# Ordering a whole diffusion step by the tile scheduler's other machine model

## The chip, the cores and the metric

The kernel runs on one NeuronCore of one Trainium2 chip. The metric is the device time of one execution in microseconds (us). Before the change the median of three runs is 1921.22 us (1920.97 to 1921.4). A difference under about 0.2% (3.8 us) counts as none.

## The reference, cut to what matters

One inference step of a two-layer backbone, for 128 context tokens and 512 latent tokens with the same weights, model width 1024. Layer 0 mixes tokens with a bidirectional state-space scan, layer 1 with differential attention; each is followed by a channel mixer of hidden width 2816.

```python
for i in range(DEPTH):                       # DEPTH = 2
    hp = modulate(xp, norm_mix_g[i], p_sh1, p_sc1)
    hs = modulate(xs, norm_mix_g[i], s_sh1, s_sc1)
    if i % N_MIXERS == 0:                    # scan in both directions, chunks of 128 tokens
        op, st = ssd_mixer(hp, h_zero, *ssd_p)
        os_, _ = ssd_mixer(hs, state_ssd[:, slot], *ssd_p)
    else:                                    # 8 heads, each with two softmax maps
        op = diff_out(diff_attend(qp, kp, vp, lam), att_subln_g[slot], att_out_w[slot], lam_init)
        os_ = diff_out(diff_attend(qs, k_all, v_all, lam), att_subln_g[slot], att_out_w[slot], lam_init)
    xp = xp + p_g1 * op
    xs = xs + s_g1 * os_
    xp = xp + p_g2 * conv_ffn(modulate(xp, norm_ffn_g[i], p_sh2, p_sc2), *ffn_p)
    xs = xs + s_g2 * conv_ffn(modulate(xs, norm_ffn_g[i], s_sh2, s_sc2), *ffn_p)
y = rmsnorm(xp, final_norm_g), rmsnorm(xs, final_norm_g)
```

## The kernel before, in words

**Layout.** Activations lie transposed in SBUF: 128 channels on the partitions, all 640 tokens (512 latent, 128 context) along the free axis, eight such tiles for the model width. A product with a weight matrix yields one output tile of 128 channels by 640 tokens at a time in PSUM, and each such tile has one "unit" of weights of at most 128 x 1024.

**Dense products.** A unit is loaded as float32 (`raw`, four buffers), then split in two float32r parts: ScalarE copies it to `whi` (L135), VectorE subtracts to get `wlo` (L136). Activations are split the same way. `dense_many` (L150 to L162) multiplies for every block of 128 input channels the three products hi x hi, hi x lo, lo x hi, each over two parts of the tokens, 256 columns ("A") and 384 columns ("B"), into the same PSUM tile. So a tile over eight blocks has 24 pairs of matmuls. `nextw` (L139) prefetches three units ahead and casts one unit ahead.

**Interleaving.** Everything that isn't a dense product is written as Python generators. `add` puts one in a list; `hook` (L75), called by `dense_many` after each block of input channels, moves those on that are due. What a generator yields is the number of hooks until it goes on. In this way the text of the program mixes the scan of a group, a head's attention, the norms and the modulation rows into the stream of dense products:

```python
for wt, x, s0, s1 in ((wh, h[k][0], st, False), (wh, h[k][1], False, False), (wl, h[k][0], False, sp)):
    for p in parts:
        c0, c1 = HALF[p]
        self.mm(ps[:m, COL0[p] + c0:COL0[p] + c1], wt, x[:, c0:c1], s0, s1)
self.hook()
```

**Stages, in the order of the text.**
- *Start* (`first_tiles`, L366): inputs, constants and the first modulation rows (`modp`, tiles `mp`, 32 transfers) are loaded on SP's queue; the first norm; the first three dense tiles.
- *Scan layer* (`ssd`, L836): for each of four groups six tiles x, B, C and four tiles z, with the scan of the group before (`ssd_group`, L669: transposes `xtp`, states `st`, decays `r`, outputs `yp`) mixed in; then the output projection `po`.
- *First channel mixer* (`ffn`, L521): 44 up tiles with a convolution over tokens on VectorE and ScalarE (`ca`, `cv`, `uraw`), then products `ml`, `mh`, and 24 down tiles `po` in three sub-blocks. `mod_rest` (L479) computes the modulation of layer 1 meanwhile, on VectorE: 48 tiles `mw` of weights are loaded and multiplied twice each (L501).
- *Attention* (`attention`, L1073): eight heads, each with dense tiles q, k, v; the scores `sl`, the softmax (`sm`, `e`) and the weighted sum (`wt`, `ov`) of one head are mixed into the dense tiles of the next. The output projection begins after six heads.
- *Second channel mixer*, as the first, without `mod_rest`; then the final norm and the stores (`final_task`, L1102).

**Who sets the order.** The text only gives a program order. When the context of L1273 closes, the tile scheduler makes of it one queue for each engine (PE, DVE, ACT, POOL and SP, which issues nearly all transfers). It plays the program on a machine model: whenever an engine of the model is free, it is given the earliest instruction in program order that the model says can run, which means that its data are there and a buffer for its result is free. The queues that come out are fixed, and semaphores are put where one engine must wait for another. On the chip each engine works its queue from the front. So an instruction that the model saw as ready sooner than the chip does holds up what stands behind it.

The lines that the prediction speaks of: L103 is every matmul but the transposes, L682 the transposes of the scan, L94 every ScalarE operation, L97 and L100 VectorE's, L123 the weight loads, L494 the loads `mw` and L501 the products made of them. Shapes tell them apart.

## Time and profile before

| | |
|---|---|
| median of three runs | 1921.22 us |
| the profiled execution's own time | 1921.78 us |
| its span, from the first to the last instruction | 1920.0 us |
| mean granted clock of TensorE | 0.993 |
| moved by DMA | 185.01 MB, mean 96 GB/s |
| DMA issues waiting longest on SP's queue | weight loads L123, 194 times, behind the cast that frees their buffer |

The profile's page gives for one execution the busy time of each engine, the chain of work that ended last, and the costliest groups of instructions. Besides it the trace answers questions by stage: how long each engine was busy between two moments, at which clock TensorE ran (1.00 is full), and on what an engine waited. A matmul's row names its output, then its moving and stationary operands by the program's names; a number with x is a count. "PEld" is TensorE's loading of stationary operands, which runs beside its matmuls. Matmuls overlap, so the mean duration of one is longer than the step from one to the next.

### The profile page before, as it was taken

The page shows a single profiled execution, that of the slowest core. Times are in us where ns is not written, and L with a number is a line of the kernel's source. Part 1 is how long each engine was busy: PE and PEld are TensorE (multiplying, and loading weights), DVE is VectorE, ACT ScalarE, POOL GpSimd, SP SyncE. Part 2 cuts the span into 40 slices and gives each one's busy share as a digit, 9 for nine tenths or more (in the row PEclk, how much of TensorE's full clock was granted, in tenths as well). Part 3 has the DMA queues.
Part 4 walks back from the last instruction along what each step waited for, and adds up shares of the span by engine and source line. Part 5 has one row for each costly group of instructions (what it writes and reads, how often), then busy time and mean ns, then how long its engine had stood idle before and what let it go on. Part 6 is the DMA issues. An engine that isn't in the chain of part 4 may idle for free.

```text
span 1920.0 us, 33586 instructions
## 1 busy us (share of the span) xinstructions
PE 1887.8 (98%) x13741; PEld 1781.4 (93%) x13741; DVE 1377.3 (72%) x2649; ACT 944.5 (49%) x1753; POOL 0.2 (0%) x4
## 2 busy tenths in 40 slices
PE   7999999999999999999999999999999999999997
PEld 4899898989989999999999989888899999999997
DVE  4779998989847999994455877788677553553554
ACT  3468585858525542343343566666446432441441
POOL 0000000000000000000000000000000000000000
PEclk9999999999999999999999999999999999999998
DMA  9612112123452556642222211111032222222211
GB/s 341 230 56 67 56 55 78 45 67 101 158 173 78 181 181 206 208 138 75 77 68 76 86 38 50 49 46 34 13 121 80 77 77 78 65 68 88 72 40 55
DMA packets 66730, 185.01 MB, mean 96 GB/s; under 512 B 8336, under 2 KB 14736, under 8 KB 66448
## 3 DMA queue, kind: packets, MB, share of 16 engines
q1 hardware_dynamic: 66000, 182.34, 29.3%
q8 instruction: 108, 1.77, 0.4%
q10 hardware_dynamic: 576, 0.52, 0.1%
q14 instruction: 46, 0.38, 0.1%
HBM read 177.06 MB, written 5.77 MB: 95 GB/s over the span
## 4 chain that ended last, share of the span: by engine, by line
PE 94%; DVE 2%; DMA 1%; ACT 1%; issue 0%; SPq 0%; DVEq 0%; ACTq 0%
PE up L103 30%; PE po L103 25%; PE z L103 6%; PE x L103 5%; PE st L103 5%; PE bc L103 3%; PE yp L103 3%; PE v L103 3%; PE q L103 2%; PE sl L103 2%; PE k L103 2%; PE ov L103 1%; PE modrow L103 1%; PE r L103 1%; PE wt L1052 1%; PE in L103 1%
## 5 line engine op out<-in xcount | busy, mean ns | idle before, releaser
L94 ACT ACTIVATE whi<-raw 128x1024 fp32r<-128x1024 f32 (+4 forms) x230 | 236.0, 1027 | 414.4 <-PE po L103 243.7
L100 DVE TENSOR_TENSOR wlo<-raw,whi 128x1024 fp32r<-128x1024 f32 (+4 forms) x230 | 270.3, 1177 | 183.8 <-ACT whi L94 178.1
L97 DVE SCALAR_TENSOR_TENSOR xr<-po,mod,xr 128x256 f32<-128x256 f32 (+2 forms) x231 | 89.0, 434 | 159.0 <-PE po L103 158.8
L103 PE MATMUL po<-mh,whi 128*128 128x256 f32 (+1 forms) x704 | 167.5, 310 | 0.0
L103 PE MATMUL po<-ml,whi 128*128 128x256 f32 (+1 forms) x704 | 167.2, 309 | 0.0
L103 PE MATMUL po<-mh,wlo 128*128 128x256 f32 (+1 forms) x704 | 167.0, 309 | 0.0
L103 PE MATMUL up<-h01h,wlo 128*128 128x256 f32 (+1 forms) x656 | 149.4, 308 | 0.0
L103 PE MATMUL up<-h11h,wlo 128*128 128x256 f32 (+1 forms) x656 | 149.4, 308 | 0.0
L103 PE MATMUL up<-h01h,whi 128*128 128x256 f32 (+1 forms) x656 | 149.3, 308 | 0.0
L103 PE MATMUL up<-h11h,whi 128*128 128x256 f32 (+1 forms) x656 | 149.3, 308 | 0.0
L103 PE MATMUL up<-h01l,whi 128*128 128x256 f32 (+1 forms) x656 | 149.3, 308 | 0.0
L103 PE MATMUL up<-h11l,whi 128*128 128x256 f32 (+1 forms) x656 | 149.3, 308 | 0.0
L103 PEld LDWEIGHTS po<-mh,whi 128*128 128x128 f32 x704 | 128.3, 188 | 0.6 <-ACT mh L94 0.4
L103 PEld LDWEIGHTS po<-mh,wlo 128*128 128x128 f32 x704 | 128.6, 188 | 0.0
L103 PEld LDWEIGHTS po<-ml,whi 128*128 128x128 f32 x704 | 128.4, 188 | 0.0
L103 PEld LDWEIGHTS up<-h01h,wlo 128*128 128x128 f32 x656 | 119.3, 188 | 0.0
L103 PEld LDWEIGHTS up<-h11h,wlo 128*128 128x128 f32 x656 | 119.3, 188 | 0.0
L103 PEld LDWEIGHTS up<-h11h,whi 128*128 128x128 f32 x656 | 119.3, 188 | 0.0
L103 PEld LDWEIGHTS up<-h01h,whi 128*128 128x128 f32 x656 | 119.3, 188 | 0.0
L103 PEld LDWEIGHTS up<-h01l,whi 128*128 128x128 f32 x656 | 119.3, 188 | 0.0
L103 PEld LDWEIGHTS up<-h11l,whi 128*128 128x128 f32 x656 | 119.2, 188 | 0.0
L97 DVE SCALAR_TENSOR_TENSOR ca<-uraw,fcw,ca 128x511 f32<-128x511 f32 (+1 forms) x176 | 85.2, 546 | 11.7 <-ACT ca L94 11.7
(505 smaller groups left out, 4469.2 us busy)
## 6 DMA issues: line engine op xcount, KB each, us to landing
raw<-in_w_up SPq DMA_DIRECT2D x88, 512.0 KB, 3.5
mw<-in_modT SPq DMA_DIRECT2D x48, 512.0 KB, 3.6
raw<-in_w_in SPq DMA_DIRECT2D x40, 512.0 KB, 3.5
raw<-in_w_dn SPq DMA_DIRECT2D x32, 448.0 KB, 3.3
raw<-in_w_qkv SPq DMA_DIRECT2D x24, 512.0 KB, 3.5
mr<-in_mod SPq DMA_DIRECT2D x44, 256.0 KB, 5.4
raw<-in_w_so SPq DMA_DIRECT2D x16, 512.0 KB, 4.1
raw<-in_w_dn SPq DMA_DIRECT2D x16, 512.0 KB, 3.7
```

Source lines behind the costliest of these rows:

```text
L94: return self.nc.scalar.activation(out, in_, func, **k)
L97: return self.nc.vector.scalar_tensor_tensor(out, in0, s, in1, op0, op1)
L100: return self.nc.vector.tensor_tensor(out, a, b, op)
L103: return self.nc.tensor.matmul(out, lhsT, rhs, start=start, stop=stop)
L1052: nc.tensor.transpose(pm[:, b * P:(b + 1) * P], ws[b][:, kc * P:(kc + 1) * P], self.ident)
```

## The change

The text of the kernel is the same. One argument of the context is set, which makes the scheduler play the program on its other machine model, a simulator of the time line of each engine and queue, in place of its default one. Both have durations and latencies of their own for each instruction and transfer; neither changes what is computed, the sizes of tiles or the number of buffers. Only the order in the five queues, which buffer of its set a tile gets, and the places of the semaphores can differ.

```diff
-    with tile.TileContext(nc) as tc:
+    with tile.TileContext(nc, schedule_with_timeline_sim=True) as tc:
         _emit(tc, **a)
```

## The prediction

> **What bounds the kernel now.** I read the page first (busy shares and the chain), then the busy time by stage, then what TensorE waited for, and last single places on the time line.
>
> ```profile
> span 1920.0 us, 33586 instructions
> PE 1887.8 (98%) x13741; PEld 1781.4 (93%) x13741; DVE 1377.3 (72%) x2649; ACT 944.5 (49%) x1753; POOL 0.2 (0%) x4
> PE 94%; DVE 2%; DMA 1%; ACT 1%; issue 0%; SPq 0%; DVEq 0%; ACTq 0%
> ```
>
> TensorE is busy in 1887.8 of 1920.0 us, and 94% of the chain that ended last is its own work. It is the bound, and 32.2 us is all that it stands idle. The profiled execution took 1921.8 us, 1.8 us more than its span; the median of the three timed runs is 1921.2 us, 0.6 us less than that, so a difference worked out in the trace is simply added to 1921.2.
>
> The next table has one row per stage (start, the scan layer, the first channel mixer, the hand-over to attention, attention with its projection, the second channel mixer, the end). Columns: length, busy time of TensorE, of its weight load, VectorE, ScalarE, GpSimd, then the granted clock, the DMA share and GB/s.
>
> ```profile
> 0.00:60.00 60.00, 48.05 (x501) 34.24 (x505) 31.77 (x67) 21.48 (x36) 0.20 (x4) 0.97 0.91 326
> 60.00:600.00 540.00, 538.43 (x4265) 485.76 (x4258) 451.88 (x905) 343.43 (x807) 0.00 (x0) 1.00 0.28 93
> 600.00:1054.00 454.00, 454.00 (x3129) 453.47 (x3127) 347.11 (x610) 179.21 (x229) 0.00 (x0) 1.00 0.42 134
> 1054.00:1080.00 26.00, 25.09 (x193) 23.82 (x194) 21.25 (x70) 12.50 (x27) 0.00 (x0) 1.00 0.23 66
> 1080.00:1440.00 360.00, 355.74 (x2443) 318.67 (x2442) 277.35 (x568) 208.93 (x427) 0.00 (x0) 0.99 0.17 54
> 1440.00:1900.00 460.00, 460.00 (x3152) 459.53 (x3150) 237.28 (x404) 178.13 (x226) 0.00 (x0) 1.00 0.21 67
> 1900.00:1920.00 20.00, 6.51 (x74) 5.90 (x72) 10.64 (x29) 0.83 (x2) 0.00 (x0) 0.70 0.38 132
> ```
>
> Of the 32.2 us idle, 11.95 lie in the first 60 us, where the DMA engines are 91% busy, and 13.49 in the last 20, where the final norm and the stores follow the last matmul. The two channel mixers, 914 us together, have no idle TensorE at all. What an order of instructions can own in the middle is 1.57 us in the scan layer, 0.91 at the hand-over and 4.26 in attention: 6.74 us.
>
> Short waits can cost more than they last. Same columns:
>
> ```profile
> 222.00:226.00 4.00, 3.21 (x21) 2.11 (x20) 3.98 (x7) 3.73 (x11) 0.00 (x0) 1.00 0.09 31
> 326.00:330.00 4.00, 3.21 (x21) 2.12 (x20) 4.00 (x6) 3.60 (x11) 0.00 (x0) 1.00 0.04 14
> 1362.00:1366.00 4.00, 2.20 (x13) 1.42 (x16) 2.88 (x7) 3.05 (x8) 0.00 (x0) 0.92 0.01 2
> 1366.00:1370.00 4.00, 4.00 (x25) 3.24 (x18) 3.33 (x10) 1.02 (x2) 0.00 (x0) 0.50 0.17 51
> 1370.00:1374.00 4.00, 4.00 (x22) 3.98 (x22) 1.95 (x7) 2.46 (x6) 0.00 (x0) 0.72 0.00 0
> 1110.00:1115.00 5.00, 4.34 (x20) 3.55 (x21) 4.60 (x10) 4.55 (x12) 0.00 (x0) 0.78 0.05 15
> 1115.00:1120.00 5.00, 5.00 (x33) 4.69 (x32) 4.18 (x8) 2.78 (x7) 0.00 (x0) 0.88 0.32 105
> ```
>
> Idle of 0.79 us near 224 and 328 left the granted clock at 1.00. Idle of 1.80 us near 1363 was followed by a clock of 0.50: 0.08 x 4 + 0.50 x 4 + 0.28 x 4 = 3.44 us of full clock lost, so that place cost 5.24 us. Near 1112, 0.66 us idle and 0.22 x 5 + 0.12 x 5 = 1.70 us of clock, 2.36 us. With 5.14 us of clock, the middle stages lose 6.74 + 5.14 = 11.9 us to places where TensorE stood waiting.
>
> **The change, part by part.** No instruction is added, dropped or resized: the same matmuls, casts and transfers come out in another order in the engines' queues, each still waiting for the same data and buffers. The scheduler gives each engine, whenever its model machine says the engine is free, the earliest instruction of the program text that the model says can run. Another model means other moments of "can run", so the order changes where engines compete, and where several jobs are open at once. That this is so already now shows inside one tile of the scan layer:
>
> ```profile
> 204.77 1.03 PE L682 MATMUL xtp<-cst,xf 128*128 128x128 f32 x8
> 205.56 0.54 PE L103 MATMUL x<-h00h,whi 128*128 128x256 f32 x2
> 208.99 0.28 PE L103 MATMUL x<-h00h,wlo 128*128 128x256 f32 x1
> 209.25 0.66 PE L682 MATMUL xtp<-cst,xf 128*128 128x128 f32 x4
> 209.66 0.42 PE L103 MATMUL x<-h00h,wlo 128*128 128x384 f32 x1
> 209.92 0.28 PE L103 MATMUL x<-h00h,whi 128*128 128x256 f32 x1
> ```
>
> Four transposes stand between the two halves of one weight tile (columns 256 and 384 of the same wlo). The text cannot put them there, since the loop of dense_many calls its hook only after all halves: the scheduler moved them.
>
> *Channel mixers (914 us).* Order matters there only if a weight cast comes late. The rows: the busiest stretch of VectorE, four pieces of the time line, two waits of SP's queue (total us, times, longest us) and one of DMA issues (count, KB, us to landing).
>
> ```profile
> 620.00:720.00 100.00, 100.00 (x684) 100.00 (x683) 99.86 (x171) 51.57 (x64) 0.00 (x0) 1.00 0.55 177
> 661.18 1.22 DVE L501 CUSTOM_DVE_ANT_0 junk<-mw,cbc 128x1024 bf16<-128x1024 f32 x1
> 662.32 1.22 DVE L100 TENSOR_TENSOR wlo<-raw,whi 128x1024 fp32r<-128x1024 f32 x1
> 662.30 0.68 ACT L94 ACTIVATE uraw<-up 128x640 f32<-128x640 f32 x1
> 668.96 0.69 ACT L94 ACTIVATE uraw<-up 128x640 f32<-128x640 f32 x1
> SPq L123 <- DVE wlo L100: 1181.6, 194, 20.9
> SPq L494 <- DVE mod L501: 118.3, 44, 5.5
> raw<-in_w_in SPq DMA_DIRECT2D x40, 512.0 KB, 3.5
> ```
>
> VectorE is full here (99.86 of 100 us), because the modulation products of the next layer are pulled forward. Yet wlo ends at 663.54 and the tile that needs it starts only when the copy-out at 668.96 shows the former one finished: 5.4 us of cover. One more modulation product ahead of it takes 1.22 us, so four in a row are needed to reach TensorE. Weight loads wait for a buffer, 6.1 us on average (1181.6 / 194), and land in about 3.5 us; the modulation loads that share SP's queue hold it at most 5.5 us, against three tiles of 7 us by which weights are fetched ahead. I take 0. If that cover went, each late cast would cost TensorE up to 1.2 us.
>
> *Start.* DMA is nearly full for 60 us, and the sum of bytes stays. One weight unit moved in SP's queue ahead of the conditioning rows that TensorE waits for costs 512 KB / 326 GB/s = 1.6 us, moved behind them it gains as much; ends -1.6 and +1.6. I take 0, as the transfers before the first dense tile stand in SP's queue in the order of the text. *End:* one chain of norm, scaling and store, 0.
>
> *Scan layer and attention (900 us).* Here eight heads and four scan groups run as chains between dense tiles, and all order-owned waits lie here. The new order draws them anew. I let half of the old ones go: -5.9 us. For the new ones I count one short wait in each of the twelve chains at the price of the rows at 222 and 326, 0.79 us: +9.5 us. One of them I let reach the clock, at the mean of the two losses seen, (1.70 + 3.44) / 2 = 2.6 us. Sum: -5.9 + 9.5 + 2.6 = +6.2 us. The ends for this term: below, every old wait goes and none comes, -11.9; above, each of the twelve costs as much as the place at 1112, 12 x 2.36 - 5.9 = +22.4. I take the value near the short waits since they are the more frequent in the trace. TensorE's waits in the middle stages (total us, times, longest us), the two longest groups:
>
> ```profile
> PE x L103 <- ACT h L94: 1.5, 2, 0.8
> PE po L103 <- ACT e L94: 1.5, 2, 1.2
> ```
>
> [...]
>
> *Cutting up.* Eight transposes in a row took 0.79 us (204.77 to 205.56). The four that split a weight tile took 209.92 - 208.99 - 0.29 = 0.64 us, where 0.29 is one undisturbed pair of halves (the row 620 to 720: 100 us for 684 matmuls, two to a pair, 7.0 us for a tile of 24 pairs). A split therefore costs about 0.64 - 0.40 = 0.24 us. Whether the new order has more or fewer is unknown: twenty either way are 4.8 us. I take 0.
>
> Forecast: 1921.2 + 6.2 = **1927 us**, 0.3% slower.
>
> **The rivals.** *The other model is nearer to this chip, and the waits go.* A wait arises where an instruction was queued too early for its data. Against the present model speak the places at 1112 and 1363; for it, that in 914 us nothing waits. With half of the loss gone and nothing new: 1921.2 - 5.9 = 1915.3; with all gone, 1909.3. It decides if the clock stays at 1.00 from 1080 to 1440 and TensorE's idle there falls below 2 us. *Nothing that can be measured.* The new waits weigh up the old ones to within 3.8 us (0.2% of 1921, about what a measurement of this kernel can tell from no change), since a machine that is full 98% hides most reordering: 1917.4 to 1925.1. In it lies the case that the argument changes no order that matters, 1921.2. *Attention falls out of step.* If in each of the eight heads the chain from scores to output is queued so that TensorE idles 1.8 us as it did once near 1363, each head pays 5.24 us: 8 x 5.24 = +42, 1963 us. It decides from the idle at which the clock halves, somewhere between 0.79 and 1.80 us in one stretch of 4 us. Against it: VectorE has 23% of attention free and ScalarE 42%.
>
> **How the numbers follow.** Forecast (slower, 1925 to 1948) 0.40; waits go 0.29; nothing measurable 0.24; attention out of step 0.07. The gain is bounded by the 11.9 us and the loss by nothing so near, which is why the slower side has more. Range: from 1909 (all waits gone) to 1948 (+22.4 and twenty splits, 1921.2 + 27.2); it leaves out the last rival and little else. The forecast's own range is 1925 to 1948. Faster by over 0.2%: 0.29, within: 0.24, slower: 0.40 + 0.07 = 0.47.
>
> **What would show it.** Right: the two mixers still without idle and about 914 us long; TensorE idle from 60 to 600 and 1080 to 1440 above the 5.8 us of now, in more places, mostly below 1 us; the granted clock of attention at 0.98 or 0.99. Wrong: idle or a lower clock inside a channel mixer (the cover of 5.4 us was eaten), a first dense tile moved by more than 1.6 us, or fewer waits than now in attention. A changed busy time of TensorE with unchanged idle would mean that the splits decide.

## The result and the profile after

The kernel after takes 2055.39 us (median of 4 runs, 2052.03 to 2057.53), beside 1921.1 us for the kernel before: a ratio of 1.0698, 95% interval 1.068 to 1.0717. It is 134 us slower; I had forecast 6.

From the page of the kernel after, the span and the busy times:

```profile
span 2050.2 us, 33659 instructions
PE 1959.2 (96%) x13741; PEld 1822.4 (89%) x13741; DVE 1379.1 (67%) x2649; ACT 938.8 (46%) x1753; POOL 0.2 (0%) x4
```

The matmuls are the same 13741, and VectorE and ScalarE do the same work. But TensorE is busy 71.4 us longer (1959.2 - 1887.8), and it idles 91.0 us in place of 32.2, 58.8 more. The span grew by 130.2, which is their sum.

By stage, first the kernel before, then after. The four rows run up to the first up tile, to the first tile q of attention, to the up tiles of the second channel mixer, and to the end; the columns are those of the stage table in the prediction.

```profile
0.00:618.50 618.50, 604.99 (x4885) 538.50 (x4886) 497.39 (x1011) 375.31 (x864) 0.20 (x4) 1.00 0.34 116
618.50:1089.30 470.80, 469.89 (x3251) 468.10 (x3250) 361.44 (x657) 187.24 (x247) 0.00 (x0) 1.00 0.41 129
1089.30:1457.80 368.50, 364.24 (x2506) 327.17 (x2505) 283.68 (x588) 213.50 (x436) 0.00 (x0) 0.99 0.17 54
1457.80:1920.00 462.20, 448.71 (x3105) 447.63 (x3103) 234.76 (x396) 168.47 (x208) 0.00 (x0) 0.99 0.22 71
```

```profile
0.00:653.80 653.80, 622.36 (x4885) 545.26 (x4886) 494.78 (x1011) 373.71 (x864) 0.20 (x4) 0.98 0.32 110
653.80:1128.50 474.70, 471.62 (x3250) 469.01 (x3249) 358.51 (x655) 183.44 (x245) 0.00 (x0) 1.00 0.41 127
1128.50:1588.60 460.10, 416.36 (x2507) 360.47 (x2506) 290.64 (x589) 212.45 (x438) 0.00 (x0) 0.93 0.14 43
1588.60:2050.20 461.60, 448.84 (x3105) 447.70 (x3103) 235.20 (x396) 169.21 (x210) 0.00 (x0) 0.99 0.23 71
```

The two rows with a channel mixer hardly moved (+3.9 with the hand-over, -0.6 with the end). Start and scan layer take 35.3 us more. Attention takes 91.6 us more, and its row splits that in three: 39.5 us of idle (43.74 against 4.26); about 28 us for the clock of 0.93 (an estimate from the two means: 0.07 x 460.1 = 32, against 0.01 x 368.5 = 4); and about 24 us in which TensorE is busy longer without either.

What TensorE waited for in attention after the change (total us, times, longest us). Before, the longest group there was po with 1.5 us:

```profile
PE obc L103 <- DVE rs_y L97: 15.5, 7, 3.2
PE op L103 <- DVE vl L100: 5.7, 6, 0.9
PE vt L935 <- DVE wTl L100: 4.0, 6, 0.9
```

**First finding: the broadcast obc.** The statistics `ms` of a head go through nine small VectorE operations (`rsqrt`) to `rs_y`, which obc needs. On the time lines of TensorE and VectorE before:

```profile
1212.59 0.48 PE L103 MATMUL ms<-osq,cst 128*32 128x160 f32 x8
...
1224.29 1.25 PE L103 MATMUL obc<-rs_y,cst 128*128 128x160 f32 x8
```

```profile
1213.13 0.33 DVE L170 TENSOR_SCALAR rs_v<-ms 128x160 f32<-128x160 f32 x1 [0.86 <-PE ms L103]
...
1218.13 0.32 DVE L97 SCALAR_TENSOR_TENSOR rs_y<-rs_a,rs_y 128x160 f32<-128x160 f32 x1
```

And after:

```profile
1245.32 0.48 PE L103 MATMUL ms<-osq,cst 128*32 128x160 f32 x8
...
1252.30 2.47 PE L103 MATMUL obc<-rs_y,cst 128*128 128x160 f32 x8 [2.48 <-DVE rs_y L97]
```

```profile
1245.86 0.33 DVE L170 TENSOR_SCALAR rs_v<-ms 128x160 f32<-128x160 f32 x1 [0.40 <-PE ms L103]
...
1251.83 0.33 DVE L97 SCALAR_TENSOR_TENSOR rs_y<-rs_a,rs_y 128x160 f32<-128x160 f32 x1
```

VectorE takes about as long (1213.13 to 1218.45, 5.3 us; 1245.86 to 1252.16, 6.3 us), with other operations in between both times. What changed is TensorE's queue: 11.7 us lay between the statistics and the broadcast, now 7.0 us, of which 2.48 is waiting. Behind obc stand the dense matmuls of v, which need nothing from it.

**Second finding: a clump at the end of q.** TensorE after, from the last dense matmul of q (1278.73) to the first of k:

```profile
1280.55 0.49 PE L103 MATMUL ov<-wTh,vh 128*128 128x512 f32 x1 [0.22 <-ACT wTh L94]
1281.91 0.66 PE L935 MATMUL vt<-cst,v 128*128 128x128 f32 x4 [0.87 <-DVE wTl L100]
...
1283.98 0.49 PE L103 MATMUL op<-wpT,vp 128*128 128x128 f32 x2 [0.94 <-DVE vl L100]
1284.71 0.56 PE L103 MATMUL k<-h10h,whi 128*128 128x256 f32 x2 [0.24 <-ACT e L94]
```

The steps wt, vt and op go through one PSUM bank, so vt waits until VectorE has read wt out of it (0.87 us) and op until it has read vt (0.94). The first wait is that of ov for its operand wTh (0.22), the last that of k for the PSUM tile of a score block (0.24); 2.27 us together. Before, dense matmuls stood between these steps, and attention's idle was 4.26 us in all.

**Third finding: matmuls that ran side by side.** A score block `sl` is twelve matmuls over 64 rows, six for each softmax map, on the two halves of the rows. Before, and then after:

```profile
1204.13 0.56 PE L103 MATMUL sl<-kh,qh 64*128 64x320 f32 x4
1204.52 0.46 PE L103 MATMUL sl<-kl,qh 64*128 64x320 f32 x4
1204.81 0.46 PE L103 MATMUL sl<-kh,ql 64*128 64x320 f32 x4
1205.20 0.56 PE L103 MATMUL q<-h10h,whi 128*128 128x256 f32 x2
```

```profile
1265.76 0.55 PE L103 MATMUL sl<-kh,qh 64*128 64x320 f32 x2
1266.16 0.45 PE L103 MATMUL sl<-kl,qh 64*128 64x320 f32 x2
1266.45 0.45 PE L103 MATMUL sl<-kh,ql 64*128 64x320 f32 x2
1266.83 0.56 PE L103 MATMUL q<-h10h,whi 128*128 128x256 f32 x2
```

Twelve took 1.07 us before (1204.13 to 1205.20); after, six alone take 1.07 us (1265.76 to 1266.83), and the next six come later at no lower price. Counted on the time lines, twelve at a time, other matmuls stand among the twelve in 23 of 32 blocks, in 6 before.

**What the order looks like.** I counted in the two built queues, for heads 1 to 6, behind how many more dense matmuls of q, k and v a step stands than in the text:

| step | wt | ov | vt | op | ms | obc | sl |
|---|---|---|---|---|---|---|---|
| before | 1.9 | 1.0 | 1.1 | 0.8 | 0.0 | 7.8 | 0.0 |
| after | 27.1 | 31.3 | 32.2 | 23.0 | 43.7 | 10.8 | 8.5 |

Before, attention all but follows the text. After, the steps of the chain are put off and obc is not, so the distance that the text gives (`yield 7`) is gone.

**Theories.** P: TensorE's own order costs, by obc (O), by the clumps (C) and by score matmuls that no longer run side by side (S). V: VectorE's and ScalarE's order makes results late, whatever TensorE's order. L: what costs is that the chain comes late at all.

### The profile page after: what moved, and what is told of

Its sections match the earlier page's. It is cut to its first block, busy times and chain, and to the rows that moved or that the text cites. A ratio compares the mean times of both kernels' runs of the same rounds, so it can differ in the third digit from the quotient of the medians.

```text
span 2050.2 us, 33659 instructions
## 1 busy us (share of the span) xinstructions
PE 1959.2 (96%) x13741; PEld 1822.4 (89%) x13741; DVE 1379.1 (67%) x2649; ACT 938.8 (46%) x1753; POOL 0.2 (0%) x4
## 4 chain that ended last, share of the span: by engine, by line
PE 90%; DVE 5%; ACT 2%; DMA 1%; issue 1%; SPq 0%; DVEq 0%; ACTq 0%
PE up L103 28%; PE po L103 23%; PE z L103 6%; PE x L103 5%; PE st L103 4%; PE bc L103 3%; PE v L103 3%; PE q L103 3%; PE sl L103 3%; PE k L103 2%; PE yp L103 2%; PE modrow L103 1%; PE in L103 1%; DVE wlo L100 1%; PE obc L103 1%; PE r L103 1%
## 5 line engine op out<-in xcount | busy, mean ns | idle before, releaser
L97 DVE SCALAR_TENSOR_TENSOR cv<-uraw,fcw,cv 128x511 f32<-128x511 f32 (+1 forms) x176 | 87.2, 549 | 10.0 <-ACT cv L94 10.0
```

Of the source, the lines that this page charges most:

```text
L97: return self.nc.vector.scalar_tensor_tensor(out, in0, s, in1, op0, op1)
```

## The experiments

A time without an interval is a single one. The kernel before, beside it on the same chip, took 1923.2, 1919.5, 1921.3 and 1922.6 us in the four groups of runs.

### Whose order it is

Edges are added behind the text that hold a queue to the order recorded from the kernel before or after; the other queues are ordered by the scheduler.

```diff
         Step(ctx, tc, a).run()
+        _replay(tc)
+def _replay(tc):
...
+        for p, n in zip(q, q[1:]):
+            tc.add_manual_dep(n, p.name, info, reason="replay")
```

*With the argument, TensorE as before.* 

> The argument is set, and TensorE's queue alone is held to the order that it has in the kernel before; VectorE, ScalarE and SyncE are ordered by the other model as it sees fit under that. Theory P (the matmuls' order itself is what costs: chain matmuls stand too early or in a clump in TensorE's in-order queue, and the score matmuls lose their pairing): nearly all comes back, 1921 to 1945 us, TensorE busy about 1888 to 1895 us. Theory V (VectorE's and ScalarE's order costs: results such as rs_y come late whatever TensorE's order is): little comes back, 2020 to 2060 us, with the waits for rs_y as long as after the change. Half by each: about 1985 us.

*Without, TensorE as after.* 

> The argument is not set, and TensorE's queue alone is held to the order that it has in the kernel after; the old model orders the other engines. Theory P: the loss is there without the argument, 2030 to 2060 us, TensorE busy about 1950 to 1960 us. Theory V: 1921 to 1950 us.

*With, VectorE and ScalarE as before.* 

> The argument is set, and VectorE's and ScalarE's queues are held to their order in the kernel before; TensorE and SyncE are ordered by the other model. Theory P: the loss stays for the most part, 2000 to 2060 us. Theory V: 1921 to 1950 us. A value between, near 1980, would mean that the model chooses TensorE's order well once the vector results come in the old order, so that the two orders belong together.

*Without, VectorE and ScalarE as after.* 

> The argument is not set, and VectorE's and ScalarE's queues are held to their order in the kernel after; the old model orders TensorE and SyncE. Theory P: 1921 to 1960 us. Theory V: 2030 to 2060 us.

Measured, with the stages read from the first and last starts of the tiles:

| kernel | us | start and scan layer | attention |
|---|---|---|---|
| before | 1921 | 618.5 | 368.5 |
| after | 2055 | 653.8 | 460.1 |
| with, TensorE as before | 1968.1 | 651.2 | 377.2 |
| without, TensorE as after | 2071.1 | 664.8 | 463.6 |
| with, VectorE and ScalarE as before | 2093.9 | 690.9 | 465.3 |
| without, VectorE and ScalarE as after | 2083.5 | 670.6 | 471.6 |

None of the four times lies in a range that a theory had named, so the stages have to be read one by one. In attention, TensorE's order carries the loss under either model: with the old order 83 of the 91.6 us are back, with the new one all of them are lost. V as stated falls there: the old order of VectorE and ScalarE brings nothing back by itself. But P was too simple: their new order alone is as dear, 2083.5 where P gave at most 1960. The time line of that run shows that the old model then orders TensorE to fit: vt stands some 30 dense matmuls later than in the kernel before, op 23, obc 3, and 22 score blocks are cut. The orders belong together. In start and scan layer no single queue brings the time back.

*With the argument, the three engines as before in attention alone* (the same edges, for attention's instructions only).

> The argument is set; in attention alone, from its first dense tile to the second channel mixer, TensorE's, VectorE's and ScalarE's queues are held to their order in the kernel before. If the stages' losses add up, attention gives back its 96 us and the start and scan layer keep their 35: 1955 to 1965 us. If attention's loss depends on what the stage before leaves behind, more than 1975 us.

Measured 1963.5 us, attention 368.1 us. The losses of the stages add up. SyncE's queue was left to the other model here, so its order has no part in what attention loses.

### The parts, one at a time

*obc later in the text, with the argument.*

```diff
-        bc = yield from self.rms_bcast(lambda: self.wide("obc"), [sq], 0, T, P, 4 if hd == 7 else 7)
+        bc = yield from self.rms_bcast(lambda: self.wide("obc"), [sq], 0, T, P, 4 if hd == 7 else 11)
```

> The argument is set; one number of the text is changed, the hooks between the statistics and the broadcast obc of an attention head, from 7 to 11, so that obc stands in TensorE's queue behind 35 matmuls of the tile v in place of ahead of it. Theory O (the wait at obc, 2.5 us per head and the half clock behind it, is a cost of its own): the waits for rs_y go and 20 to 35 us come back, 2020 to 2035 us. Rival (the late chain just waits somewhere else): 2045 to 2060 us, with as much idle at other matmuls of the chain.

Measured 2029.1 us, 26 less than after. The waits of TensorE there:

```profile
PE ov L103 <- ACT wTh L94: 5.2, 16, 1.4
...
PE obc L103 <- DVE rs_y L97: 3.2, 1, 3.2
```

Six of the seven waits at obc are gone, and theory O holds. Attention's idle fell by 8.7 us only, since other steps wait longer (ov for wTh 2.9 us after the change, 5.2 here; wt for wTl 1.4 and 4.8), and its clock rose from 0.93 to 0.96, some 15 us by the two means. This order also cuts the score blocks less, `sl` is busy 6.4 us less than after, so not all of the 26 is obc's.

*The weighted sum five hooks later, without the argument.*

```diff
-        self.tails[hd] = self.add(self.att_tail(hd, w, ws, vs, o, pool), 1 if last else 2)
+        self.tails[hd] = self.add(self.att_tail(hd, w, ws, vs, o, pool), 1 if last else 7)
...
-        bc = yield from self.rms_bcast(lambda: self.wide("obc"), [sq], 0, T, P, 4 if hd == 7 else 7)
+        bc = yield from self.rms_bcast(lambda: self.wide("obc"), [sq], 0, T, P, 4 if hd == 7 else 2)
```

> The argument is not set; in the text the weighted sum of each head but the last begins five hooks later (30 dense matmuls, about as much as the transposes wt and the products ov slide in the kernel after, 27 and 31), and obc stays where it was. The old model keeps this later chain spread evenly among the dense matmuls. Theory L (the chain's lateness by itself costs, since what it frees comes late): half or more of attention's loss, 1970 to 2020 us. Theory C (it is not lateness, but that steps of the chain stand next to each other with no dense matmul between them): 1918 to 1935 us.

Measured 1922.2 us, 2.7 more than the kernel before beside it. L falls: a chain later by nearly 30 dense matmuls, but spread among them, loses nothing like half of attention's 91.6 us. It is not shown to be free: in the same run `sl` is busy 6.8 us less (44.0), and obc waits 4.9 us for rs_y.

*Four clumps in the old order.* The edges again, for TensorE in attention, with the old order changed in four heads (the lines sketch the queue and are not code):

```diff
-q x12, wt x4, ov x3, sl x12, q x6, vt x4, q x6, ov x3, q x1, op x1, q x5, sl x12
+q x12, sl x12, q x18, sl x12, wt x4, ov x3, vt x4, ov x3, op x1
```

> The argument is not set; TensorE's queue in attention is held to its order in the kernel before, but that in four of the eight heads fifteen small matmuls of the chain (wt, ov, vt, ov, op), which stand between dense matmuls there, stand behind one another with no dense matmul between, as they do at the end of q in the kernel after. Theory C (such a clump lets each step's round trip to ScalarE and VectorE be seen): about 2.3 us idle per head, as the kernel after shows in its clumps, and up to as much again by the clock: 1929 to 1941 us. Rival (clumps cost nothing by themselves): 1919 to 1924 us.

Measured 1934.2 us, 12.9 more than the kernel before beside it. The longest waits are now those of vt for wTl (6.7 us in four). The stretch from 1080 to 1480 us, before and with the clumps:

```profile
1080.00:1480.00 400.00, 395.74 (x2711) 358.67 (x2710) 307.45 (x633) 234.15 (x466) 0.00 (x0) 0.99 0.18 56
```

```profile
1080.00:1480.00 400.00, 384.19 (x2620) 343.12 (x2619) 298.60 (x618) 228.21 (x458) 0.00 (x0) 0.99 0.17 52
```

Idle went from 4.26 to 15.81 us, 2.9 us per clump, at the same mean clock of 0.99: the third clump was followed by a clock of 0.50 (rows in the last section), as the place near 1363 was before. C holds, without the clock's part that I had allowed for.

*The twelve score matmuls six and six, in the old order* (the edges again, all three engines held to it otherwise; sl0 and sl1 are the tiles of the two maps).

```diff
-sl0 x1, sl1 x1, sl0 x1, sl1 x1, ...
+sl0 x6, sl1 x6
```

> The argument is not set; TensorE's, VectorE's and ScalarE's queues are held to their order in the kernel before, but for one thing: the twelve score matmuls sl of each of the 32 blocks are issued six for the one score tile and then six for the other, as they mostly are in the kernel after, where the kernel before alternates between the two tiles in most of them. Theory S (the lost pairing is the 3 us per head by which sl is busier): eight heads by 3.0 us, 24 us, so 1940 to 1950 us with TensorE busy about 24 us more and no more idle. Rival (sl is only busier because the clock is lower there): 1921 to 1926 us.

Measured 1929.2 us, 9.7 more, but `sl` is busy only 3.1 us more (rows below). Attention is 6.5 us longer, of which 3.0 are busy TensorE and 3.5 idle, 2.7 of them in one wait of sl. Theory S as stated fails: six and six that stand next to each other still overlap, twelve in 1.47 us on the time line. Then what matters is whether something stands between them:

```diff
-            for j, (x, kk) in enumerate(((qh, kh), (qh, kl), (ql, kh))):
-                for c0 in (0, 320):
-                    for r, hf in zip(rs, half):
+            for r, hf in zip(rs, half):
+                for j, (x, kk) in enumerate(((qh, kh), (qh, kl), (ql, kh))):
+                    for c0 in (0, 320):
                         self.mm(r[:, 192 + c0:192 + c0 + 320], x[hf, qb], kk[hf, c0:c0 + 320], j == 0, j == 2)
+                if r is rs[0]:
+                    yield 1
...
-            yield 2
+            yield 1
```

> The argument is not set; in the text the six score matmuls sl of the second score tile come one hook (six dense matmuls) after the six of the first, and what follows keeps its distance. Theory S2 (matmuls on different halves of the rows run side by side only when they stand next to each other in the queue; six alone take 1.07 us, as long as twelve that alternate): 32 blocks by up to 1.07 us, less what the blocks that are imperfectly paired in the kernel before already pay: sl busy 28 to 34 us more, 1945 to 1956 us. Rival (the 20 us that sl grew by in the kernel after are clock): sl within 5 us of before, under 1930 us.

Measured 1942.3 us, 21 more than before. TensorE's busy time for `sl` over the whole run (the number ahead of x384; then its weight loads, VectorE, ScalarE, clock, DMA) before, after, with six and six adjacent, and with six dense matmuls between:

```profile
0.00:2100.00 2100.00, 50.86 (x384) 38.80 (x384) 50.23 (x64) 54.45 (x128) 0.99 0.27 88
```

```profile
0.00:2100.00 2100.00, 71.06 (x384) 52.63 (x384) 51.86 (x64) 54.99 (x128) 0.98 0.27 88
```

```profile
0.00:2100.00 2100.00, 53.95 (x384) 44.75 (x384) 50.23 (x64) 54.40 (x128) 0.99 0.27 88
```

```profile
0.00:2100.00 2100.00, 73.25 (x384) 55.71 (x384) 52.50 (x64) 56.37 (x128) 1.00 0.28 88
```

Apart, `sl` grows by 22.4 us at a clock of 1.00 with no new wait, and the run by 21. It is less than the 28 I had named (in the kernel before, too, not all pairs start together: 116 of 192 within 0.04 us), but it is the size of what the kernel after lost on sl, 20.2 us. S2 holds.

*The modulation rows of the start.* Four matmuls `modrow`, one for each 32 output rows, run side by side as well. The trace shows each as two records: eight of the text (x16) take 1.92 us before, 0.96 for four, and after, one that stands alone (x2) takes 1.04.

```profile
59.20 1.92 PE L103 MATMUL modrow<-mr,s 128*32 128x512 f32 x16
```

```profile
50.28 1.04 PE L103 MATMUL modrow<-mr,s 128*32 128x512 f32 x2
```

With the argument, the edges hold TensorE up to attention to its new order, but that five such fours are put together again. One of them:

```diff
-modrow, 15 others, modrow, 12 others, modrow, 6 others, modrow
+modrow x4
```

> The argument is set; up to attention TensorE's queue is held to its order in the kernel after, but that each four modulation matmuls modrow (one for each quarter of the columns) which the other model cut up by dense matmuls stand together again (five such fours, of sixteen). Theory Q (four run side by side in the time of one, and alone each takes as long as four, about 0.5 us): modrow busy 5 to 10 us less, 2045 to 2051 us. Rival (modrow grew by the low clock of the start): unchanged, 2053 to 2060 us.

Measured 2051.0 us, 4.4 less than the median after, but only 1 us under its fastest run (2052.03 to 2057.53), so that this time alone would not settle it. TensorE's time for modrow, before, after, and with the five fours mended:

```profile
0.00:2100.00 2100.00, 28.02 (x384) 10.01 (x384) 2.31 (x6) 0.99 0.27 88
```

```profile
0.00:2100.00 2100.00, 40.46 (x384) 11.54 (x384) 2.30 (x6) 0.98 0.27 88
```

```profile
0.00:2100.00 2100.00, 34.58 (x384) 10.81 (x384) 2.31 (x6) 0.98 0.28 88
```

5.9 of the 12.4 us are back, and the first matmul x<-h00h starts at 63.0 us in place of 68.2: Q holds at its lower end, though the price of one alone is about 1 us and not the half that I had named. The rest of modrow's growth was not taken apart.

### A version faster than both

The weighted sum five hooks later, with obc keeping its seven hooks (the first of the two edits of that run alone, without the argument).

> The argument is not set; as in the kernel with the weighted sum five hooks later, and obc keeps its seven hooks behind the statistics, so that it is later too. Waits for rs_y at obc should go (4.9 us there), and the score matmuls are all paired: 1914 to 1920 us. Rival (what is spared in TensorE's work is idle elsewhere, as the end of attention comes later): 1920 to 1925 us.

Measured 1916.67 us (10 runs, 1915.26 to 1918.33) against 1921.29 (13 runs): ratio 0.9974, interval 0.9964 to 0.9983. The gain of 4.6 us is little more than the 0.2% below which a difference counts as none. `sl` is busy 43.4 us in place of 50.9, as more of its matmuls alternate: on the time line 166 of 192 pairs start within 0.04 us of each other, 116 in the kernel before and 39 in the kernel after.

### Why the model puts the chain off

*The same text, with the argument.* 

> The argument is set, and the text is that in which the weighted sum of a head begins five hooks later and obc with it (it ran in about 1917 us without the argument). If what attention loses belongs to the model alone, whatever the text, the loss stays: 2040 to 2060 us. If it comes from what this text leaves the model to move, the later chain and the distance at obc spare it most of that: 1985 to 2015 us, with no waits at obc, and sl busy 10 us less than in the kernel after.

Measured 2034.7 us, between the two: 20.7 less than after. sl is busy 63.2 us (7.9 less), but attention's clock is lower still, 0.91 from 1136 to 1568.6 us, and the waits are others:

```profile
PE sl L103 <- ACT e L94: 10.2, 10, 1.3
...
PE obc L103 <- DVE rs_y L97: 3.2, 1, 3.2
```

More distance spares the waits at obc, one of seven is left, but most of the loss stays with the model, which places other steps too close in this text.

*A shorter round trip through the chain's PSUM bank.* The low part wTl of the transposed attention weights is left out and the high part multiplied twice, so that the matmuls stay as many and VectorE has one operation less behind each copy out of the bank.

```diff
             hi = pool.tile([P, TS], F32R, tag="wTh", name="wTh", bufs=2)
-            lo = pool.tile([P, TS], F32R, tag="wTl", name="wTl", bufs=2)
+            lo = hi
             self.act(hi, pm, AF.Copy)
-            self.tt(lo, pm, hi.bitcast(F32), ALU.subtract)
```

> The argument is set; the low part of the transposed attention weights (wTl, one VectorE operation behind ScalarE's copy out of the single bank of PSUM that wt, vt, op and ms share) is left out, and the high part is multiplied twice in its place, so the matmuls are as many. In the queue as built wt slides 9 dense matmuls behind its place in the text in place of 27, and ov 14 in place of 31; sl stays cut up. If the round trip through that bank is why the model puts the chain off, and the put-off chain is what costs idle time: 15 to 35 us less than after, 2020 to 2040 us, with the waits before vt and op gone. If not: 2045 to 2055 us.

> The same text as the run without wTl, and the argument not set: the control. 1915 to 1922 us, since nothing in attention waited for wTl in the kernel before; were it under 1910 us, the spared VectorE work would be a gain by itself.

Measured 2045.2 us with the argument and 1913.0 without: 10.2 less than after and 9.5 less than the kernel before beside it, where I had expected 1915 at least. The gain is about the same without the argument, so it is no part of what the argument costs. What brings it was not taken apart; it lies in TensorE's busy time in attention (11.9 and 9.0 us less). Attention's idle with the argument did not fall (45.6 us, 43.7 after): new waits took the place of the old, 12.0 us at wt alone for `w`. The round trip is not why the loss is there. Why the other model puts these steps off stays open.

## Why the prediction was wrong

- **Channel mixers and end, 0: right.** From the first to the last matmul up<-h·h,whi the first mixer takes 392.9 us (394.2 before), the second 394.1 both times. The cover of 5.4 us for late casts held: TensorE is busy in 446.20 of the 446.20 us from 653.8 to 1100 after the change. (It would take five more products of 1.22 us to eat that cover, not the four that I wrote: 5.4 / 1.22 = 4.4.)
- **Scan layer and attention: the step that failed** is "I count one short wait in each of the twelve chains at the price of the rows at 222 and 326, 0.79 us: +9.5 us". In attention a head came to 91.6 / 8 = 11.5 us, with 39.5 us of new idle in the stage, and the clock, for which I had let one place pay 2.6 us, came to about 28 by the estimate above. I priced the new waits by those that the old order had left over, which were small because that order was good, and took VectorE's 23% and ScalarE's 42% of free time as cover. The free engines did not cover the chain of dependent steps; the dense matmuls that stood between its steps in TensorE's queue did (in the run with four clumps TensorE idled 2.9 us more for each), and the new order took them away at the end of q. The line "a machine that is full 98% hides most reordering" was the wrong way round.
- **The rival "Attention falls out of step"** had what was seen, idle in the heads together with a low clock, and named 42 us for it, with a chance of 0.07. In attention it was 39.5 us of idle and, by the same estimate, about 28 of clock, 67 together.
- **Cutting up: taken at 0, wrong.** I priced a split at 0.24 us of hand-over and let gains and losses cancel. What was measured is the price of matmuls that no longer run side by side: 1.07 us for a score block whose halves stand apart, 20.2 us more for sl in the kernel after, and 1.04 us for a modrow that stands alone, where four together take 0.96. I had not asked what runs side by side. My mark for it, more busy time, came true together with more idle.
- **Start, at most 1.6 us either way: wrong.** The first matmul x<-h00h starts at 68.2 us in place of 56.7. TensorE is busy all the same from 50 to 68, with the tiles `in` and with modulation rows, many of them cut up: up to that first matmul modrow takes 24.2 us (294 records) in place of 12.6 (256), and `in` 24.5 in place of 22.4.
- **Sum.** Of attention's 91.6 us the single parts account for some 55: obc 20 (26.3 less the 6.4 by which sl shrank there), sl 21, and clumps 14, which is what op, vt, ov and k wait in the kernel after (5.7 + 4.0 + 2.9 + 1.2; at the 2.9 us per clump of the run with four, eight heads would give 23). This is an estimate from separate runs. The rest was not taken apart. Of the 35 us of start and scan layer, modrow is 12.4, and the cuts that were mended 5.9 of these. Idle grew there from 13.51 to 31.44 us. Over half of that growth lies in two kinds of wait in the scan layer that the kernel before does not have:

```profile
PE r L103 <- DVE xf L97: 5.4, 2, 2.8
PE gbc L103 <- DVE rs_y L97: 4.4, 1, 4.4
```

The second is a broadcast that waits for `rsqrt`, as obc does. No run tests either, and no single queue's old order brings this stage back, so that its cause stays open.

## What to carry to other kernels

A scheduler's order is a resource like a buffer: where one engine is full and small dependent steps ride in its in-order queue, check in the built queue that dense work still stands between a step and its successor (2.9 us of idle per clump here), and that matmuls which ran side by side still stand next to each other (1.07 us per score block here). Spare time on the other engines, 23% of VectorE's and 42% of ScalarE's in attention, said nothing about that. To find who owns a loss, replay the recorded order of one queue under the other setting and compare stage by stage, but expect the orders of the engines to depend on each other.

## What was unexpected of the hardware

The order of the score matmuls over 64 rows, on the two halves, set their time: twelve take 1.07 us alternating (the kernel before), 1.47 us as six and six next to each other (the run with the old order), and 2.14 us as two sixes apart, 1.07 us each (the kernel after). With six dense matmuls between the sixes, `sl` is busy 73.25 us in the run, beside 50.86 before. The four modrow, one for each 32 output rows, gave the same picture: 0.96 us for four, 1.04 for one alone.

The granted clock did not follow the sum of the idle. After the change, around the wait at obc and around the clump:

```profile
1249.00:1253.00 4.00, 1.25 (x6) 1.04 (x7) 3.76 (x11) 2.78 (x8) 0.00 (x0) 0.89 0.41 122
1253.00:1257.00 4.00, 4.00 (x21) 4.00 (x21) 3.99 (x7) 1.23 (x2) 0.00 (x0) 0.68 0.08 26
1279.00:1283.00 4.00, 2.91 (x16) 1.68 (x14) 1.83 (x2) 1.89 (x3) 0.00 (x0) 1.00 0.16 22
1283.00:1287.00 4.00, 2.81 (x18) 2.58 (x18) 2.25 (x7) 4.00 (x12) 0.00 (x0) 1.00 0.33 126
```

With 2.75 us of idle, 2.48 of it in one piece, the clock went to 0.50 from 1252.11 to 1255.52 us (obc's eight records took 2.47 us in place of 1.25); with 2.28 us in four pieces it stayed at 1.00. Nor did the same idle always go with the same clock. In the run with four clumps, the second clump and the third:

```profile
1211.60:1215.60 4.00, 1.62 (x9) 1.07 (x9) 2.58 (x5) 1.56 (x4) 0.00 (x0) 1.00 0.00 0
1215.60:1219.60 4.00, 3.57 (x29) 2.93 (x29) 1.32 (x4) 2.96 (x8) 0.00 (x0) 1.00 0.06 16
1251.40:1255.40 4.00, 1.64 (x8) 1.16 (x9) 2.48 (x5) 1.66 (x4) 0.00 (x0) 0.96 0.00 0
1255.40:1259.40 4.00, 3.63 (x14) 3.34 (x15) 1.18 (x3) 2.98 (x8) 0.00 (x0) 0.50 0.07 18
```

Both idle about 2.4 us in 4, and no wait of vt for wTl in that run is longer than 1.7 us; of the two, only the third was followed by a clock of 0.50. So the sum per 4 us, for which the prediction put the limit between 0.79 and 1.80 us, did not decide by itself in these runs. The longest wait of attention in the kernel after was 3.2 us, and its clock was 0.93. In that trace attention has 13 stretches at a clock of 0.50. They begin whole multiples of 3.41 us apart (1187.26, 1204.32 and 1252.11 us are three of the starts, 5 and 14 times 3.41 us apart); nine last 3.41 us, three 6.83 and one 10.24. Whether the moment at which TensorE idles decides along with the length was not tested.
